# Batched x times y transposed on one core: longer DMA runs, 64-column weight tiles, deeper load prefetch, permutations moved to the transposed operands

## The chip, the core and the metric

The kernel runs on one core of one Trainium2 chip. The metric is device microseconds (us) of one execution; the median of three runs is given. A core has five engines: TensorE (PE, matmuls and transposes), VectorE (DVE), ScalarE (ACT), GpSimd (POOL) and SyncE (SP, which only issues transfers here). Sixteen DMA engines move data between HBM and the on-chip memory SBUF. Matmul results land in PSUM and are copied from there by DVE or ACT.

## The reference

```python
batch, n_heads, seq_t, seq_s, channels = 8, 12, 512, 512, 64      # x, y float32
np.einsum('bhtc,bhsc->bhts', x, y).astype(np.float32)
```

For each of 96 heads the output is a 512 x 512 float32 matrix, x times y transposed over 64 channels. Inputs are 12.6 MB each, the output is 100.7 MB.

## The kernel before, in words

The 96 heads are worked off in 24 groups of four (the loop at line 50). Everything below happens once per group, written out in program order; each engine takes its own instructions in that order, and waits are inserted where one needs another's result or a buffer that is still in use. Buffers rotate: three of each kind for loaded inputs, converted inputs, transposed inputs and outputs, four PSUM buffers for transposes and four for matmuls.

*Loads (lines 54 and 57, issued by SP).* Rows of a head are dealt out so that partition p holds the four consecutive rows 4p to 4p+3. One load brings 512 KB of x or y, as runs of 1 KB: four rows of 64 channels of 4 bytes, for 128 partitions and four heads.

*Conversion (lines 65 and 66, ACT).* Float32 becomes bf16. The heads of a pair are laid side by side, so that a 128-column block holds row 4p+tl of both heads.

*Transposes (lines 73 and 77, PE; copies at 74 and 78, DVE).* Each 128 x 128 block is turned over by PE into PSUM and copied to `xT` or `yT` by DVE. The first head of a pair then has its 64 channels on partitions 0 to 63, the second on 64 to 127. There are 16 transposes and 16 copies of 128 elements per partition in a group.

*Matmuls (line 87, PE).* For each head and each of four row sets there is one matmul: a 64 x 128 weight tile from `xT`, and all 512 columns of `yT`. That makes 16 per group, each filling one PSUM buffer of 128 x 512. In program order two heads of a pair follow each other, so the array rows 0 to 63 are used by four matmuls, then rows 64 to 127 by four.

*Output copies (line 96 on ACT, line 98 on DVE, alternating).* The columns of a matmul come in the order (sl, ps), while the output wants ps outside and sl inside. The copy from PSUM to `ot` undoes that: it reads in order and writes every fourth word.

*Store (line 99, issued by POOL).* One transfer of 4 MB per group, in runs of 8 KB: four rows of 512 columns per partition and head. It waits until all 16 copies of its group are done.

Of the kernel before, what the change touches and what calls it, by code (L numbers as in the profile page):

```python
# [1 line left out]

# [5 lines left out]


@with_exitstack
def kernel(
    ctx: ExitStack,
    tc: tile.TileContext,
    x: bass.AP,
    y: bass.AP,
    out: bass.AP,
):
    nc = tc.nc
    B, H, T, C = x.shape  # L20
    _, _, S, _ = y.shape
    BH = B * H
    P = 128
    TL = T // P
    SL = S // P
    fp32 = mybir.dt.float32
    bf16 = mybir.dt.bfloat16

    assert C * 2 == P

    NPAIR = 2
    BB = NPAIR * 2
    NB = BH // BB

    xv = x.rearrange("b h (p tl) c -> (b h) p tl c", p=P)
    yv = y.rearrange("b h (p sl) c -> (b h) p sl c", p=P)
    ov = out.rearrange("b h (p tl) s -> (b h) p tl s", p=P)

    const = ctx.enter_context(tc.tile_pool(name="const", bufs=1))
    ident = const.tile([P, P], bf16)  # L40
    make_identity(nc, ident)

    lpool = ctx.enter_context(tc.tile_pool(name="lpool", bufs=3))
    bpool = ctx.enter_context(tc.tile_pool(name="bpool", bufs=3))
    tpool = ctx.enter_context(tc.tile_pool(name="tpool", bufs=3))
    opool = ctx.enter_context(tc.tile_pool(name="opool", bufs=3))
    ptpool = ctx.enter_context(tc.tile_pool(name="ptpsum", bufs=4, space=bass.MemoryType.PSUM))
    pmpool = ctx.enter_context(tc.tile_pool(name="pmpsum", bufs=4, space=bass.MemoryType.PSUM))

    for nb in range(NB):  # L50
        bh0 = nb * BB
        xs = lpool.tile([P, BB, TL, C], fp32)
        ys = lpool.tile([P, BB, SL, C], fp32)
        nc.sync.dma_start(
            xs, xv[bh0:bh0 + BB].rearrange("bb p tl c -> p bb tl c")
        )
        nc.sync.dma_start(
            ys, yv[bh0:bh0 + BB].rearrange("bb p sl c -> p bb sl c")
        )
        xb = bpool.tile([P, NPAIR, TL, 2, C], bf16)  # L60
        yb = bpool.tile([P, NPAIR, SL, 2, C], bf16)
        for pr in range(NPAIR):
            xsv = xs[:, 2 * pr:2 * pr + 2].rearrange("p two tl c -> p tl two c")
            ysv = ys[:, 2 * pr:2 * pr + 2].rearrange("p two sl c -> p sl two c")
            nc.scalar.activation(xb[:, pr], xsv, mybir.ActivationFunctionType.Copy)  # L65
            nc.scalar.activation(yb[:, pr], ysv, mybir.ActivationFunctionType.Copy)  # L66

        xT = tpool.tile([P, NPAIR, TL, P], bf16)
        yT = tpool.tile([P, NPAIR, SL, P], bf16)
        for pr in range(NPAIR):  # L70
            for tl in range(TL):
                pt = ptpool.tile([P, P], bf16)
                nc.tensor.transpose(pt, xb[:, pr, tl, :, :], ident)  # L73
                nc.vector.tensor_copy(xT[:, pr, tl, :], pt)  # L74
            for sl in range(SL):
                pt = ptpool.tile([P, P], bf16)
                nc.tensor.transpose(pt, yb[:, pr, sl, :, :], ident)  # L77
                nc.vector.tensor_copy(yT[:, pr, sl, :], pt)  # L78

        ot = opool.tile([P, BB, TL, S], fp32)  # L80
        for pr in range(NPAIR):
            for two in range(2):
                bb = pr * 2 + two
                yTf = yT[two * C:(two + 1) * C, pr].rearrange("c sl p -> c (sl p)")
                for tl in range(TL):
                    pm = pmpool.tile([P, S], fp32)
                    nc.tensor.matmul(  # L87
                        pm,
                        xT[two * C:(two + 1) * C, pr, tl, :],
                        yTf,  # L90
                        start=True, stop=True,
                    )
                    pmv = pm.rearrange("p (sl ps) -> p sl ps", sl=SL)
                    otv = ot[:, bb, tl, :].rearrange("p (ps sl) -> p sl ps", sl=SL)
                    if tl % 2 == 0:
                        nc.scalar.activation(otv, pmv, mybir.ActivationFunctionType.Copy)  # L96
                    else:
                        nc.vector.tensor_copy(otv, pmv)  # L98
        nc.gpsimd.dma_start(  # L99
            ov[bh0:bh0 + BB].rearrange("bb p tl s -> p bb tl s"), ot  # L100
        )


# [1 line left out]
_INS = ['x', 'y']  # L105
_OUTS = [((8, 12, 512, 512), 'float32')]


# [23 lines left out]
```

## Time and profile before

| | us |
|---|---|
| median of three runs (321.52, 322.62, 323.64) | 322.62 |
| profiled execution, span from first to last instruction | 323.1 |

| | |
|---|---|
| loads | 48, of 512 KB |
| stores | 24, of 4 MB |
| HBM read / written | 25.17 MB / 100.66 MB |
| mean rate over the span | 390 GB/s |
| instructions | 2677 |

How to read the lines that follow in this document. Busy rows give microseconds and the share of the span for each engine; PEld is PE's weight loads. A group row has line, engine, operation, output and input tiles with shape, then a count, total busy time, mean ns of one, and the idle time before it with what ended it. A timeline row has start, duration, engine, line, operation and a count of instructions merged into the row. A window row has the stretch and its length, the busy time of PE, PEld, DVE, ACT and POOL with instruction counts, the granted share of the TensorE clock, the DMA share (mean busy share of the 16 DMA engines; over 1 where packets of one engine overlap) and GB/s. A queue row has packets, MB and the time that its packets took as a share of 16 engines' span. q1 carries what SP issues, q0 what POOL issues. Ends of matmuls are modelled, starts are recorded.

### The profile page before, as it was taken

How to read it: one execution, taken by the hardware profiler on the slowest of the kernel's cores; microseconds unless marked ns; L12 is line 12 of the kernel's file. 1: busy time of each engine (PE TensorE's matmuls, PEld its weight loads, DVE VectorE, ACT ScalarE, POOL GpSimd, SP SyncE). 2: the span in 40 equal slices, each digit the busy share in tenths (PEclk: the TensorE clock that was granted, in tenths of full speed). 3: DMA queues.
4: the chain of work that ended last, by engine and by line, in shares of the span. 5: the costliest groups of instructions: out<-in, count | busy, mean ns of one | idle time of the engine just before them, and what ended most of it. 6: DMA issues, size and time to landing. Idle time of an engine off the chain costs nothing. (4 is left out here: it accounts for less than half of the span.)

```text
span 323.1 us, 2677 instructions
## 1 busy us (share of the span) xinstructions
PE 235.5 (73%) x768; PEld 76.6 (24%) x768; DVE 237.3 (73%) x576; ACT 233.3 (72%) x289; POOL 18.7 (6%) x30
## 2 busy tenths in 40 slices
PE   2578878878386697787887877977966999889300
PEld 1122222224032213313312313312312223222000
DVE  2488797797287877877886886886867899999500
ACT  4798678684669688687697697696686976699400
POOL 0010000000000000000000000000000000000000
DMA  7959999999999999999999999999998699999995
GB/s 249 353 180 405 365 420 419 421 422 417 410 331 406 349 424 415 417 420 417 409 428 417 411 426 415 415 426 417 420 425 350 290 418 392 397 402 414 417 422 247
DMA packets 38031, 126.01 MB, mean 390 GB/s; under 512 B 1152, under 2 KB 25728, under 8 KB 25728
## 3 DMA queue, kind: packets, MB, share of 16 engines
q0 software_dynamic: 12672, 100.66, 74.5%
q1 hardware_dynamic: 25344, 25.17, 23.0%
q8 instruction: 6, 0.10, 0.1%
q14 instruction: 9, 0.07, 0.1%
HBM read 25.17 MB, written 100.66 MB: 389 GB/s over the span
## 5 line engine op out<-in xcount | busy, mean ns | idle before, releaser
L87 PE MATMUL pm<-yT,xT 64*128 64x512 bf16 x384 | 179.7, 603 | 54.3 <-ACT ot L96 51.2
L98 DVE COPY ot<-pm 128x512 f32<-128x512 f32 x192 | 184.4, 1080 | 36.4 <-PE pm L87 36.2
L96 ACT ACTIVATE ot<-pm 128x512 f32<-128x512 f32 x192 | 184.4, 1119 | 12.2 <-PE pm L87 12.1
L87 PEld LDWEIGHTS <-xT 64*128 64x128 bf16 x384 | 38.7, 111 | 166.8 <-issue 130.7
L65 ACT ACTIVATE xb<-xs 128x512 bf16<-128x512 f32 x48 | 28.6, 629 | 48.1 <-PE pt L73 25.7
L78 DVE COPY yT<-pt 128x128 bf16<-128x128 bf16 x192 | 30.8, 218 | 23.7 <-PE pt L77 23.7
L77 PE MATMUL pt<-ident,yb 128*128 128x128 bf16 x192 | 32.6, 283 | 7.1 <-DVE xT L74 6.3
L73 PE MATMUL pt<-ident,xb 128*128 128x128 bf16 x192 | 32.4, 271 | 4.9 <-ACT xb L65 4.9
L66 ACT ACTIVATE yb<-ys 128x512 bf16<-128x512 f32 x48 | 28.6, 629 | 8.3 <-DMA ys<-in_y_dram 7.0
L99 POOL DMA_DIRECT2D out_dram<-ot x24 | 18.0, 752 | 285.1 <-DVE xT L74 208.1
L74 DVE COPY xT<-pt 128x128 bf16<-128x128 bf16 x192 | 29.8, 226 | 5.8 <-PE pt L73 5.8
L77 PEld LDWEIGHTS <-yb 128*128 128x128 bf16 x192 | 18.5, 114 | 35.6 <-issue 31.0
L73 PEld LDWEIGHTS <-xb 128*128 128x128 bf16 x192 | 20.2, 111 | 22.1 <-issue 12.1
L65 ACT ACT_TABLE_LOAD x1 | 1.3, 1283 | 0.7 <-PEq L116 0.7
masks.py:199 POOL TENSOR_SCALAR_AFFINE_SELECT ident<-ident 128x128 bf16<-128x128 bf16 x1 | 0.3, 290 | 0.1
masks.py:197 POOL MEMSET ident<- 128x128 bf16 x1 | 0.2, 205 | 0.3 <-POOLq L116 0.3
L116 POOL MEMSET const-float32-0.0<- 128x1 f32 x1 | 0.1, 99 | 0.2 <-issue 0.2
L116 POOL MEMSET const-bfloat16-1.0<- 128x1 bf16 x1 | 0.1, 102 | 0.0
L116 POOL MEMSET const-uint8-127<- 128x1 uint8 x1 | 0.1, 102 | 0.0
L116 POOL MEMSET const-float32-1.0<- 128x1 f32 x1 | 0.1, 99 | 0.0
## 6 DMA issues: line engine op xcount, KB each, us to landing
out_dram<-ot POOLq DMA_DIRECT2D x24, 4096.0 KB, 15.9
xs<-in_x_dram SPq DMA_DIRECT2D x24, 512.0 KB, 12.7
ys<-in_y_dram SPq DMA_DIRECT2D x24, 512.0 KB, 14.6
```

Of the source, the lines that this page charges most:

```text
L65: nc.scalar.activation(xb[:, pr], xsv, mybir.ActivationFunctionType.Copy)
L66: nc.scalar.activation(yb[:, pr], ysv, mybir.ActivationFunctionType.Copy)
L73: nc.tensor.transpose(pt, xb[:, pr, tl, :, :], ident)
L74: nc.vector.tensor_copy(xT[:, pr, tl, :], pt)
L77: nc.tensor.transpose(pt, yb[:, pr, sl, :, :], ident)
L78: nc.vector.tensor_copy(yT[:, pr, sl, :], pt)
L87: nc.tensor.matmul(pm, xT[two * C:(two + 1) * C, pr, tl, :], yTf, start=True, stop=True,)
L96: nc.scalar.activation(otv, pmv, mybir.ActivationFunctionType.Copy)
L98: nc.vector.tensor_copy(otv, pmv)
L99: nc.gpsimd.dma_start(ov[bh0:bh0 + BB].rearrange("bb p tl s -> p bb tl s"), ot)
L116: nc = _bacc.Bacc("TRN2", target_bir_lowering=False, num_devices=1)
```

## The change

The group stays four heads, with a different deal of rows. A load is read as a flat 512 KB: partition p gets 4 KB, 16 consecutive rows of head p // 32. A store covers two heads, 2 MB; each partition writes eight consecutive output rows, 16 KB.

Weight tiles have 64 columns: 32 partitions of a head times two row octets. Each matmul fills 64 partitions of a PSUM buffer that is now 128 x 2 x 512, so two heads and two row parities, four matmuls, share a buffer. Even rows have their channels on partitions 0 to 63 and odd rows on 64 to 127. The columns of y are needed on both halves, so y is written twice side by side in the conversion and transposed in 16 blocks, x in 8. The order of columns and rows is put right in the copies of transposed blocks (three copies of 128 x 1024 per group, two on DVE and one on ACT); the output copies read and write in order, 1024 elements at a time.

Conversions move from ACT to POOL. All transfers are issued by SP, loads for six groups ahead of everything else, then each group's loads behind the conversion that frees their buffers. Buffers: six for loads, two for converted and transposed inputs, eight for outputs, two PSUM buffers for transposes and three for matmuls. The preparation of the next group is a generator whose steps are interleaved with the output tiles of the present one. The first and the last output tile are stored in two halves.

The deleted loop is the one printed above; the new code:

```diff
-    xv = x.rearrange("b h (p tl) c -> (b h) p tl c", p=P)
-    yv = y.rearrange("b h (p sl) c -> (b h) p sl c", p=P)
-    ov = out.rearrange("b h (p tl) s -> (b h) p tl s", p=P)
+    G = 4
+    Q = P // G
+    R = T // Q
+    NG = B * H // G
+    K = R // 2
+    HP = 2
+    I = R // 2
...
+    xv = x.rearrange("b h t c -> (b h t c)").rearrange("(g p n) -> g p n", p=P, n=R * C)
+    yv = y.rearrange("b h t c -> (b h t c)").rearrange("(g p n) -> g p n", p=P, n=R * C)
+    ov = out.rearrange("b h t s -> (b h t s)").rearrange("(g a p n) -> g a p n", a=G // HP, p=P, n=I * S)
...
+    lpool = ctx.enter_context(tc.tile_pool(name="lpool", bufs=6))
+    bpool = ctx.enter_context(tc.tile_pool(name="bpool", bufs=2))
+    tpool = ctx.enter_context(tc.tile_pool(name="tpool", bufs=2))
+    opool = ctx.enter_context(tc.tile_pool(name="opool", bufs=8))
+    ptpool = ctx.enter_context(tc.tile_pool(name="ptpsum", bufs=2, space=bass.MemoryType.PSUM))
+    pmpool = ctx.enter_context(tc.tile_pool(name="pmpsum", bufs=3, space=bass.MemoryType.PSUM))
+
+    loaded = {}
+
+    def load(g):
+        xs = lpool.tile([P, R * C], fp32)
+        ys = lpool.tile([P, R * C], fp32)
+        nc.sync.dma_start(ys, yv[g])
+        nc.sync.dma_start(xs, xv[g])
+        loaded[g] = (xs, ys)
+
+    for g in range(6):
+        load(g)
...
+    def prepare(g, made):
+
+        xs, ys = loaded.pop(g)
+        yb = bpool.tile([P, R, 2, C], bf16)
+        nc.gpsimd.tensor_copy(
+            yb, ys.rearrange("p (r c) -> p r c", c=C).unsqueeze(2).to_broadcast([P, R, 2, C])
         )
+        xb = bpool.tile([P, R * C], bf16)
+        nc.gpsimd.tensor_copy(xb, xs)
+        if g + 6 < NG:
+            load(g + 6)
+        yield
+        yT = tpool.tile([P, G * Q, R], bf16)
+        xT = tpool.tile([P, K // 2, P, 2], bf16)
+        for half in range(2):
+            pt = ptpool.tile([P, K, P], bf16)
+            for k in range(K):
+                nc.tensor.transpose(
+                    pt[:, k, :], yb[:, half * K + k].rearrange("p a c -> p (a c)"), ident
+                )
+            dst = yT[:, :, half * K:(half + 1) * K]
+            src = pt.rearrange("p k n -> p n k")
+            if half == 0:
+                nc.vector.tensor_copy(dst, src)
+            else:
+                nc.scalar.activation(dst, src, mybir.ActivationFunctionType.Copy)
+            yield
+        pt = ptpool.tile([P, K, P], bf16)
+        for k in range(K):
+            nc.tensor.transpose(pt[:, k, :], xb[:, k * P:(k + 1) * P], ident)
+        nc.vector.tensor_copy(
+            xT.rearrange("p i n e -> p i e n"), pt.rearrange("p (e i) n -> p i e n", e=2)
         )
+        made[g] = (xT, yT.rearrange("p n k -> p (n k)"))
+        yield
...
+    made = {}
+    for _ in prepare(0, made):
+        pass
+    for g in range(NG):
+        xT, yT = made.pop(g)
+        steps = prepare(g + 1, made) if g + 1 < NG else iter(())
+        for hp in range(G // HP):
+            ot = opool.tile([P, I, S], fp32)
+            edge = (g == 0 and hp == 0) or (g == NG - 1 and hp == 1)
+            for i2 in range(I // 2):
+                if i2 % 2 == 0:
+                    next(steps, None)
+                pm = pmpool.tile([P, 2, S], fp32)
+                for h2 in range(HP):
+                    h = hp * HP + h2
+                    for par in range(2):
+                        nc.tensor.matmul(
+                            pm[h2 * 64:(h2 + 1) * 64, par, :],
+                            xT[par * C:(par + 1) * C, i2, h * Q:(h + 1) * Q, :].rearrange("c q e -> c (q e)"),
+                            yT[par * C:(par + 1) * C, h * S:(h + 1) * S],
+                            start=True, stop=True,
+                        )
+                if i2 % 2 == 0:
+                    nc.scalar.activation(ot[:, 2 * i2:2 * i2 + 2, :], pm, mybir.ActivationFunctionType.Copy)
+                else:
+                    nc.vector.tensor_copy(ot[:, 2 * i2:2 * i2 + 2, :], pm)
+                if edge and i2 % 2 == 1:
+                    a, b = (2 * i2 - 2) * S, (2 * i2 + 2) * S
+                    nc.sync.dma_start(ov[g, hp][:, a:b], ot.rearrange("p r s -> p (r s)")[:, a:b])
+            if not edge:
+                nc.sync.dma_start(ov[g, hp], ot.rearrange("p r s -> p (r s)"))
```

More of the change, by code (lines that the diff above doesn't have):

```diff
@@ L21 @@
     _, _, S, _ = y.shape
-    BH = B * H
     P = 128
-    TL = T // P
-    SL = S // P
+    G = 4
[5 more added lines that the diff above has]
+    I = R // 2
     fp32 = mybir.dt.float32
     bf16 = mybir.dt.bfloat16
[L29 to L33, printed above, removed]
-    xv = x.rearrange("b h (p tl) c -> (b h) p tl c", p=P)
-    yv = y.rearrange("b h (p sl) c -> (b h) p sl c", p=P)
-    ov = out.rearrange("b h (p tl) s -> (b h) p tl s", p=P)
@@ L39 @@
-    const = ctx.enter_context(tc.tile_pool(name="const", bufs=1))
+    assert C * 2 == P and S == T and R == 16
+    xv = x.rearrange("b h t c -> (b h t c)").rearrange("(g p n) -> g p n", p=P, n=R * C)
+    yv = y.rearrange("b h t c -> (b h t c)").rearrange("(g p n) -> g p n", p=P, n=R * C)
+    ov = out.rearrange("b h t s -> (b h t s)").rearrange("(g a p n) -> g a p n", a=G // HP, p=P, n=I * S)
+    const = ctx.enter_context(tc.tile_pool(name="const", bufs=1))
+    lpool = ctx.enter_context(tc.tile_pool(name="lpool", bufs=6))
@@ L40 @@
+    for g in range(6):
+        load(g)
     ident = const.tile([P, P], bf16)
     make_identity(nc, ident)
[L43 to L55, printed above, removed]
-        )
-        nc.sync.dma_start(
-            ys, yv[bh0:bh0 + BB].rearrange("bb p sl c -> p bb sl c")
-        )
[L60 to L101, printed above, removed]
```

## The prediction

> **What bounds the kernel now.** I read the page's totals first, then its slices and DMA queues.
>
> ```profile
> PE 235.5 (73%) x768; PEld 76.6 (24%) x768; DVE 237.3 (73%) x576; ACT 233.3 (72%) x289; POOL 18.7 (6%) x30
> ...
> DMA packets 38031, 126.01 MB, mean 390 GB/s; under 512 B 1152, under 2 KB 25728, under 8 KB 25728
> ...
> q0 software_dynamic: 12672, 100.66, 74.5%
> q1 hardware_dynamic: 25344, 25.17, 23.0%
> ```
>
> No compute engine passes 73%, while the two queues take 97.5% of the 16 DMA engines' time. Each transfer ends in a small packet per engine (1152 in all), so q0 has 12672 - 384 = 12288 data packets of 8 KB and q1 25344 - 768 = 24576 of 1 KB. In queue time one 8 KB packet costs 0.745 x 16 x 323.1 / 12288 = 313.4 ns, one 1 KB packet 0.230 x 16 x 323.1 / 24576 = 48.4 ns. Summed and spread over 16 engines that is 315.0 us of the 323.1.
>
> Then the windows: busy time of each engine, granted clock, DMA share and GB/s.
>
> ```profile
> 0.00:2.40 2.40, 0.00 (x0) 0.00 (x0) 0.00 (x0) 1.28 (x1) 0.70 (x6) 1.00 0.13 29
> 5.00:18.00 13.00, 8.15 (x32) 2.77 (x33) 6.90 (x21) 9.93 (x16) 0.00 (x0) 1.00 1.06 344
> 18.00:23.50 5.50, 3.91 (x14) 1.28 (x12) 5.07 (x16) 5.50 (x10) 0.88 (x1) 1.00 0.46 143
> 204.00:219.00 15.00, 12.23 (x39) 3.78 (x37) 12.25 (x31) 11.22 (x14) 0.83 (x2) 1.00 1.02 421
> 240.00:260.00 20.00, 16.95 (x60) 5.92 (x58) 16.30 (x46) 15.30 (x18) 1.49 (x2) 1.00 0.81 338
> 304.00:319.00 15.00, 0.00 (x0) 0.00 (x0) 0.00 (x0) 0.00 (x0) 0.45 (x1) 1.00 1.00 416
> 319.00:323.10 4.10, 0.00 (x0) 0.00 (x0) 0.00 (x0) 0.00 (x0) 0.00 (x0) 1.00 0.21 86
> ```
>
> Nothing moves for 2.4 us at the start. At the end 86 GB/s over 4.1 us is 0.35 MB, 0.8 us of work, so some 3.3 us are empty. Between them are stretches of 344 GB/s with 1 KB loads alone, 421 with both kinds, 416 with 8 KB stores alone, and holes. The first hole, 18.0 to 23.5, follows three groups of loads: input buffers are full, and the first store only goes out at 22.41. The later one (240 to 260, 338 GB/s) comes when no loads are left to fill the time between stores. In the timeline of that phase:
>
> ```profile
> 22.41 0.88 POOL L99 DMA_DIRECT2D out_dram<-ot  x1 [21.11 <-DVE yT L78]
> ...
> 259.62 7.47 DVE L98 COPY ot<-pm 128x512 f32<-128x512 f32 x8
> 260.59 6.88 ACT L96 ACTIVATE ot<-pm 128x512 f32<-128x512 f32 x7 [2.23 <-PE pm L87]
> 262.57 3.68 PE L87 MATMUL pm<-yT,xT 64*128 64x512 bf16 x8 [0.23 <-DVE ot L98]
> 267.63 0.75 POOL L99 DMA_DIRECT2D out_dram<-ot  x1 [9.79 <-DVE xT L74]
> 278.00 0.75 POOL L99 DMA_DIRECT2D out_dram<-ot  x1 [9.62 <-DVE xT L74]
> ```
>
> Stores leave 10.37 us apart, while 4.19 MB at 416 GB/s take 10.1: there compute sets the pace. So the time is DMA work first and compute where its slack has run out. Both matter for the change.
>
> **The change, part by part.** *DMA run lengths.* Bytes stay; packets become 6144 loads of 4 KB and 6144 stores of 16 KB. Through my two prices goes a line of (313.4 - 48.4) / 7168 = 0.0370 ns per byte plus 10.5 ns per packet. It gives 162.0 ns for 4 KB (between two measured sizes) and 616.3 ns for 16 KB (beyond them). The sum is 6144 x (162.0 + 616.3) / 16 = 298.9 us, 16.1 less than 315.0; loads give 12.1 of it, stores 4.0. Two independent rows fit the prices: 416 GB/s alone is 315 ns per 8 KB, and 344 GB/s at a share of 1.06 is 48 ns of wall per 1 KB. The only 16 KB packets of this trace are instruction fetches:
>
> ```profile
> q8 instruction: 6, 0.10, 0.1%
> ```
>
> At 0.1% of 16 x 323.1 us, six of them took roughly 0.9 us each, beside store traffic. That is the dear bound; the cheap one is that packets overlap as in the rows with shares of 1.02, 298.9 / 1.02 = 293.0 us. I take the line, since stores alone run at a share of 1.00.
>
> *Ends and holes.* 2.4 us and 3.3 us stay. The first hole should close: six groups are requested at once, a seventh while the first is prepared. Per group the loads cost 256 x 162.0 / 16 = 2.6 us, so DMA is fed until 2.4 + 7 x 2.6 = 20.6. The first store, now half of a two-head tile, can be ready before that; the landing of the first inputs and the small POOL operations give its date:
>
> ```profile
> 4.25 0.63 ACT L65 ACTIVATE xb<-xs 128x512 bf16<-128x512 f32 x1 [2.23 <-DMA xs<-in_x_dram]
> 5.72 0.63 ACT L66 ACTIVATE yb<-ys 128x512 bf16<-128x512 f32 x1 [0.84 <-DMA ys<-in_y_dram]
> ...
> masks.py:199 POOL TENSOR_SCALAR_AFFINE_SELECT ident<-ident 128x128 bf16<-128x128 bf16 x1 | 0.3, 290 | 0.1
> masks.py:197 POOL MEMSET ident<- 128x128 bf16 x1 | 0.2, 205 | 0.3 <-POOLq L116 0.3
> L116 POOL MEMSET const-float32-0.0<- 128x1 f32 x1 | 0.1, 99 | 0.2 <-issue 0.2
> ```
>
> *POOL.* It now converts 2048 + 1024 elements per partition and group. The trace shows no conversion there. From 1 to 128 elements a memset grows 106 ns and the select 191 over the memset of one element: 0.83 and 1.50 ns per element, so 2.6 to 4.6 us per group. I take 4.6, as a copy reads like the select does. It no longer waits for stores. The Trainium skill's page "GPSIMD Engine Reference" (section 3.1) measures about 2.6 cycles per element for a two-input add at 1.2 GHz, and section 4.1 advises against elementwise work there; by that figure, an estimate, a group would take 6.7 us. No run here shows a conversion on POOL; the sum would be the same by either.
>
> *Copies on DVE and ACT.*
>
> ```profile
> 268.29 0.62 DVE L78 COPY yT<-pt 128x128 bf16<-128x128 bf16 x4 [0.78 <-PE pt L77]
> 159.42 1.15 ACT L65 ACTIVATE xb<-xs 128x512 bf16<-128x512 f32 x2 [2.77 <-issue]
> ```
>
> Today's output copies write every fourth word and cost 7.47 / 8 = 0.93 us per 512 on DVE, 0.98 on ACT. The new ones write in order. In-order writes cost 0.155 us per 128 on DVE and (1.15 - 0.63) = 0.52 per 512 on ACT. For 1024 elements: DVE between 1.24 and 1.87, ACT between 1.04 and 1.97. I take the low ends, the rows with in-order writes. The permutation moves into the copies of transposed x and y (1024 elements each, strided reads or writes); I give these the high ends, and note that strided PSUM reads are not in the trace. Per group DVE does 4 x 1.24 + 2 x 1.87 = 8.7 us, ACT 4 x 1.04 + 1.97 = 6.1; with strided prices throughout 11.2 and 9.8.
>
> *PE.* Transposes go from 16 to 24 per group, matmuls from 16 to 32, each with 64 weight columns and 512 moving columns.
>
> ```profile
> 15.98 0.61 PE L87 MATMUL pm<-yT,xT 64*128 64x512 bf16 x2
> 159.25 0.66 PE L77 MATMUL pt<-ident,yb 128*128 128x128 bf16 x4
> 259.75 0.27 PE L73 MATMUL pt<-ident,xb 128*128 128x128 bf16 x1
> L87 PE MATMUL pm<-yT,xT 64*128 64x512 bf16 x384 | 179.7, 603 | 54.3 <-ACT ot L96 51.2
> L87 PEld LDWEIGHTS <-xT 64*128 64x128 bf16 x384 | 38.7, 111 | 166.8 <-issue 130.7
> ```
>
> Matmuls on the same rows of the array follow at about (3.68 - 0.60) / 7 = 0.44 us. The first row here is the pair in program order where the rows change from 64-127 to 0-63: two take the time of one. The change alternates rows at each matmul. If only such pairs overlap, 16 x 0.44 = 7.0 us; if column halves overlap too, 3.5; if nothing does, 14.1. Transposes at (0.66 - 0.27) / 3 = 0.13 add 3.1; weight loads at half of 0.111, if none hides, 1.8. So 6.6 to 11.9 us, and 19.0 without any overlap. I take pairs with half the loads hidden, 11.0. The skill's page "TensorEngine Tiling (Array Packing)" (section Tiling Modes) says that different tiles run matmuls and weight loads in parallel, and that changing the mode drains the engine, which speaks against three blocks of transposes per group among tiled matmuls. The 15.98 row agrees on rows; no run here shows column tiles, and by the page PE would need 6.6 us and the drains.
>
> *Does compute keep up?* DMA needs 298.9 / 24 = 12.45 us per group with loads, 256 x 616.3 / 16 = 9.86 without. While loads run, every estimate lies under 12.45, so stores pile up: with eight output tiles of 4.9 us each, seven can stand ahead of the one in transfer, 34 us. In the last six groups PE at 11.0 is late by 1.1 each, 7 us, paid from the lead. Hence compute costs nothing. The date of the first store: y at 4.3 (now loaded first), conversions to 4.3 + 4.6 = 8.9, three blocks of eight transposes with copies about 5, two output tiles 2.5, so about 16.5 against 20.6.
>
> *SP.*
>
> ```profile
> 160.59 0.37 SPq L54 DMA_DIRECT2D xs<-in_x_dram  x1
> L99 POOL DMA_DIRECT2D out_dram<-ot x24 | 18.0, 752 | 285.1 <-DVE xT L74 208.1
> ```
>
> It issues 48 loads and 50 stores (0.37 us each, 36 us in all) where POOL issued 24 at 0.75. Loads of a later group wait for POOL's conversion, and the store behind them in program order waits with them. That is covered by transfers already queued; a POOL late by more than the queue's backlog would leave DMA empty.
>
> Sum: 2.4 + 298.9 + 3.3 = 304.6. The same account for before gives 320.7 against its 323.1, the rest being holes less overlaps. The profiled span is within 0.5 us of the median, 322.6. I predict **304.5 us**.
>
> **The rivals.** (1) *More overlap*: 293.0 + 5.7 = 298.7. For it: shares of 1.02 to 1.06; against: 1.00 with stores alone. (2) *Run length buys little*: long descriptors are cut, or bytes and not packets cost. With stores still cut at 8 KB, 6144 x 162.0 / 16 + 240.7 + 5.7 = 308.6; with loads unchanged as well, 315.0 + 5.7 = 320.7. For it: the line rests on two sizes and 16 KB lies outside; against: 344 beside 416 GB/s. (3) *Matmuls don't overlap*: PE at 19.0 us per group becomes the bound, 16 + 24 x 19.0 + 5 = 477; without exposed weight loads 433. It decides from 12.6 us per group, where 20 + 24 x 12.6 equals today's time. For it: column tiles are nowhere in the trace; against: the 15.98 row. (4) *POOL conversion is the bound*: needs over 12.6 / 3072 = 4.1 ns per element; at three times the select's slope, 4.5, it is 20 + 24 x 13.8 = 351. Against: both POOL rows. (5) *The strided copies are*: DVE needs (12.6 - 5.0) / 2 = 3.8 us for each, twice my price; at 4.0 it is 20 + 24 x 13.0 = 332.
>
> **How the numbers follow.** A measurement here tells about 1% from no change, 319.4 to 325.8. Chances: forecast (301 to 309) 0.62, rival 1 0.08, rival 2 0.15 (0.12 of it below 319.4, 0.03 within 1%), rival 3 0.06, rival 4 0.05, rival 5 0.04 (half of it within 1%). Faster 0.82, same 0.05, slower 0.13. The range leaves out the slower cases and the top of rival 2: 298 to 316, with rival 1 at its low end.
>
> **What would show it.** Right: 4 KB packets near 162 ns and 16 KB near 616 in queue time, a DMA share of at least 0.98 from 3 us to the end, no hole at 18 to 23, a first store before 20.6, output copies near 1.2 and 1.0 us, PE pairs starting together. Wrong: more than 12288 data packets, a share that falls while PE, POOL or DVE is full, or SP's stores waiting behind a load for POOL.

## The result and the profile after

The changed kernel takes 308.95 us, the median of four runs (306.84 to 309.27), beside 322.19 for the kernel before, timed with it: a ratio of 0.955, 95% interval 0.949 to 0.961. The profiled run is one of 308.88 us with a span of 307.1, so 1.8 us lie around the span. I had predicted 304.5 within 298 to 316. Direction and cause hold; the time is 4.4 us longer than the sum.

First the page of the changed kernel: totals, DMA and GB/s in 40 slices, packets and queues.

```profile
PE 154.7 (50%) x1344; PEld 82.8 (27%) x1344; DVE 172.9 (56%) x144; ACT 117.3 (38%) x121; POOL 70.6 (23%) x54
...
DMA  7999999999999999999999999999999999999970
GB/s 277 415 400 438 420 418 429 419 436 414 423 436 416 425 428 428 425 426 423 433 428 417 437 427 424 430 425 431 428 427 433 428 425 438 429 427 435 430 327 42
DMA packets 14127, 126.04 MB, mean 410 GB/s; under 512 B 1568, under 2 KB 1568, under 8 KB 7712
...
q1 hardware_dynamic: 14112, 125.84, 97.4%
q8 instruction: 10, 0.16, 0.2%
```

The holes are gone: after the first slice the rate stays at 400 GB/s or more until the last two. Queue time is 0.974 x 307.1 = 299.1 us; the line through the two old packet sizes had said 298.9. Now the windows that answer to those of before.

```profile
5.00:18.00 13.00, 10.45 (x92) 6.36 (x93) 8.54 (x8) 5.58 (x6) 10.54 (x8) 1.00 1.02 404
18.00:23.50 5.50, 4.61 (x56) 2.41 (x56) 5.50 (x6) 4.81 (x6) 2.88 (x2) 1.00 1.03 399
40.00:240.00 200.00, 113.61 (x948) 61.67 (x948) 122.04 (x102) 80.73 (x85) 49.76 (x34) 0.59 1.01 426
```

The last stretch in the kernel before:

```profile
40.00:240.00 200.00, 154.06 (x518) 52.09 (x517) 154.89 (x395) 151.15 (x194) 11.19 (x15) 1.00 1.02 412
```

Loads alone run at 404 GB/s instead of 344, the hole at 18.0 to 23.5 has 399 instead of 143, and the long middle 426 instead of 412. The groups of instructions show the engines with time to spare (after the bar: busy us and mean ns of one):

```profile
L125 DVE COPY ot<-pm 128x1024 f32<-128x1024 f32 x96 | 116.4, 1220 | 80.8 <-DMA out_dram<-ot 60.1
L123 ACT ACTIVATE ot<-pm 128x1024 f32<-128x1024 f32 x96 | 94.3, 1022 | 144.1 <-DMA out_dram<-ot 131.6
L68 POOL CAST yb<-ys 128x2048 bf16<-128x2048 f32 x24 | 45.4, 1893 | 138.9 <-DMA ys<-in_y_dram 108.9
L94 DVE COPY xT<-pt 128x1024 bf16<-128x1024 bf16 x24 | 31.1, 1298 | 9.5 <-PE pt L93 9.5
L87 DVE COPY yT<-pt 128x1024 bf16<-128x1024 bf16 x24 | 29.1, 1214 | 7.1 <-PE pt L81 7.1
L72 POOL CAST xb<-xs 128x1024 bf16<-128x1024 f32 x24 | 25.0, 1040 | 21.6 <-PE pt L93 21.6
L89 ACT ACTIVATE yT<-pt 128x1024 bf16<-128x1024 bf16 x24 | 24.7, 1028 | 7.0 <-PE pt L81 6.2
```

ACT, DVE and POOL mostly wait for a store or a load: DMA sets the pace. What the sum had missed is at the end. Here are the last stretches in 40 slices each, first of the kernel before (311 to 323.1, 0.30 us a slice), then of the changed one (295 to 309, 0.35 us a slice).

```profile
GB/s 406 379 406 406 433 433 406 433 406 433 433 433 433 433 433 433 433 433 406 433 406 433 433 433 379 433 433 379 379 54 27 0 0 0 0 0 0 0 0 0
```

```profile
GB/s 468 398 445 304 375 281 304 234 70 140 70 117 117 140 94 47 70 47 47 70 47 70 47 23 23 23 23 23 47 23 0 0 0 0 0 0 0 0 23 0
DMA packets 196, 1.47 MB, mean 105 GB/s; under 512 B 31, under 2 KB 31, under 8 KB 31
```

Before, all 16 DMA engines stop within a microsecond. After, they stop one by one: 23 is one 8 KB packet per slice, one engine at work. Spread evenly, at the 428 GB/s of the stretch from 240 to 260 us, the 1.47 MB would have ended at 295 + 1.47 / 0.428 = 298.4; the last engine ends at 295 + 30 x 0.35 = 305.5. That costs 7.1 us.

### The profile page after: what moved, and what is told of

Same layout as the page of the kernel before. It is cut to its first block, busy times and chain, and to the rows that moved or that the text cites. A ratio compares the mean times of both kernels' runs of the same rounds, so it can differ in the third digit from the quotient of the medians.

```text
span 307.1 us, 3408 instructions
## 1 busy us (share of the span) xinstructions
PE 154.7 (50%) x1344; PEld 82.8 (27%) x1344; DVE 172.9 (56%) x144; ACT 117.3 (38%) x121; POOL 70.6 (23%) x54
## 4 chain that ended last, share of the span: by engine, by line
DMA 78%; DVE 5%; PE 3%; issue 1%; ACT 1%; POOL 1%; SPq 0%; ACTq 0%
DMA out_dram<-ot 77%; DVE ot L125 3%; PE pm L116 1%; DVE xT L94 1%; DMA ys<-in_y_dram 1%; PE pt L81 1%; DVE yT L87 1%; ACT ot L123 1%; POOL yb L68 1%; PE pt L93 0%; SPq L130 0%; ACTq L123 0%
## 5 line engine op out<-in xcount | busy, mean ns | idle before, releaser
L125 DVE COPY ot<-pm 128x1024 f32<-128x1024 f32 x96 | 116.4, 1220 | 80.8 <-DMA out_dram<-ot 60.1
L123 ACT ACTIVATE ot<-pm 128x1024 f32<-128x1024 f32 x96 | 94.3, 1022 | 144.1 <-DMA out_dram<-ot 131.6
L116 PE MATMUL pm<-yT,xT 64*64 64x512 bf16 x768 | 95.1, 556 | 91.0 <-ACT ot L123 72.3
L68 POOL CAST yb<-ys 128x2048 bf16<-128x2048 f32 x24 | 45.4, 1893 | 138.9 <-DMA ys<-in_y_dram 108.9
L116 PEld LDWEIGHTS <-xT 64*64 64x64 bf16 x768 | 32.1, 120 | 138.8 <-issue 120.5
L81 PEld LDWEIGHTS <-yb 128*128 128x128 bf16 x384 | 34.6, 128 | 24.6 <-issue 18.2
L94 DVE COPY xT<-pt 128x1024 bf16<-128x1024 bf16 x24 | 31.1, 1298 | 9.5 <-PE pt L93 9.5
L87 DVE COPY yT<-pt 128x1024 bf16<-128x1024 bf16 x24 | 29.1, 1214 | 7.1 <-PE pt L81 7.1
L72 POOL CAST xb<-xs 128x1024 bf16<-128x1024 f32 x24 | 25.0, 1040 | 21.6 <-PE pt L93 21.6
L89 ACT ACTIVATE yT<-pt 128x1024 bf16<-128x1024 bf16 x24 | 24.7, 1028 | 7.0 <-PE pt L81 6.2
```

The lines of the kernel that those rows point to most:

```text
L68: nc.gpsimd.tensor_copy(yb, ys.rearrange("p (r c) -> p r c", c=C).unsqueeze(2).to_broadcast([P, R, 2, C]))
L72: nc.gpsimd.tensor_copy(xb, xs)
L81: nc.tensor.transpose(pt[:, k, :], yb[:, half * K + k].rearrange("p a c -> p (a c)"), ident)
L87: nc.vector.tensor_copy(dst, src)
L89: nc.scalar.activation(dst, src, mybir.ActivationFunctionType.Copy)
L94: nc.vector.tensor_copy(xT.rearrange("p i n e -> p i e n"), pt.rearrange("p (e i) n -> p i e n", e=2))
```

## The experiments

The theory after the result: the time is the packets' queue time, spread over 16 engines, plus what the slowest engine is late; compute, buffers and queues are covered. Rivals: the gain comes from prefetch depth, from the cheaper copies, or from the queue. The ratio is to the kernel before, timed beside each run. Timed together were store_8k, load_1k, more_pe and less_pe; control, load_1k_one, before_deep and wide_load; and the other four.

| run | us | ratio, 95% interval |
|---|---|---|
| control: the changed kernel again | 306.93 | 0.952, 0.949 to 0.955 |
| store_8k | 311.75 | 0.963, 0.956 to 0.969 |
| load_1k: four transfers per load | 335.98 | 1.039, 1.031 to 1.048 |
| load_1k_one: one transfer per load | 314.62 | 0.977, 0.972 to 0.982 |
| before_deep: the kernel before, deep prefetch | 318.69 | 0.989, 0.986 to 0.992 |
| small_buf | 307.61 | 0.952, 0.947 to 0.956 |
| strided_out | 306.96 | 0.950, 0.945 to 0.956 |
| pool_store | 309.95 | 0.959, 0.954 to 0.964 |
| more_pe | 309.99 | 0.958, 0.952 to 0.964 |
| less_pe | 305.99 | 0.946, 0.939 to 0.954 |
| wide_load | 308.66 | 0.957, 0.954 to 0.960 |
| no_dup | 309.21 | 0.957, 0.951 to 0.963 |

**Control.** No edit. 

> The changed kernel itself again, as the yardstick on this chip. Expected 309 (306.8 to 309.3 so far).

 It came at 306.93; with the first runs that gives the changed kernel 307 to 309.

**Store runs undone.**

```diff
-            edge = (g == 0 and hp == 0) or (g == NG - 1 and hp == 1)
+            edge = True
```

> Every output tile is stored in two transfers, each of 8 KB runs instead of 16 KB; all else is as in the changed kernel. Theory (price per packet as on the line, 8 KB = 309 to 313 ns): store packets rise from 6144 to 12288, queue time by about (12288 x 311 - 5888 x 613 - 512 x 312) / 16 = 3.3 us, the time from 309 to about 312. Rival (the longer store run brings nothing, all gain comes from loads and holes): 309 within 0.5. Second rival (two stores per tile let DMA start earlier and waits shrink): below 308.

311.75 us, ratio 0.963 beside 0.952 and 0.955 for the changed kernel: 2.5 to 3.5 us of 323, near the 3.3 that the packet price gave. The run also issues 46 transfers more; what these cost by themselves it does not show. In the middle of the run (20 to 260 us) the rate is 420 GB/s:

```profile
20.00:260.00 240.00, 138.52 (x1200) 73.79 (x1198) 154.70 (x130) 102.80 (x107) 58.50 (x40) 0.62 1.01 420
```

and in the control, at the same place:

```profile
20.00:260.00 240.00, 139.40 (x1220) 74.19 (x1217) 157.44 (x132) 105.01 (x109) 58.40 (x40) 0.63 1.01 426
```

**Load runs undone, first try.** Four transfers of 1 KB runs for each load.

```diff
-        nc.sync.dma_start(ys, yv[g])
-        nc.sync.dma_start(xs, xv[g])
+        for j in range(4):
+            nc.sync.dma_start(ys[:, j * 256:(j + 1) * 256], yv[g][:, j * 256:(j + 1) * 256])
+        for j in range(4):
+            nc.sync.dma_start(xs[:, j * 256:(j + 1) * 256], xv[g][:, j * 256:(j + 1) * 256])
```

> Each 512 KB load is cut into four transfers of 128 runs of 1 KB, as long as the runs of the kernel before; stores stay at 16 KB. Theory (the load packets set most of the gain): 24576 x 48.4 instead of 6144 x 163.4 ns over 16 engines is 74.3 instead of 62.7 us, so 11.6 us more, about 320.5. Rival (loads of 1 KB are cheap once they lie ahead in one queue with stores, packets overlapping): under 313. Issue time on SP grows by 144 x 0.33 = 48 us and should be hidden by six groups of lead.

336 us, beyond both. SP issues one transfer in 0.46 us at the start, and 128 KB per 0.46 us is 285 GB/s, so SP and not DMA sets the first 20 us. The timeline of SP and the window 5 to 20 us:

```profile
0.74 1.81 SPq L55 DMA_DIRECT2D ys<-in_y_dram  x4
```

```profile
5.00:20.00 15.00, 9.86 (x109) 6.02 (x110) 10.35 (x9) 7.36 (x8) 10.43 (x7) 1.00 0.83 260
```

That explains about 6 of the 29 us: from 2.4 to 20 us the rate was 261 GB/s against 407 in the control. Later 16 KB packets took 641 instead of 613 ns, for which no run here gives the reason. The run does not price the run length; it shows that my "issue time is hidden by the lead" fails while no lead exists yet.

**Load runs undone, second try.** One transfer, four pieces of 1 KB per partition.

```diff
-    xv = x.rearrange("b h t c -> (b h t c)").rearrange("(g p n) -> g p n", p=P, n=R * C)
+    xv = x.rearrange("b h t c -> (b h t c)").rearrange("(g j p n) -> g p j n", j=4, p=P, n=R * C // 4)
...
-        nc.sync.dma_start(xs, xv[g])
+        nc.sync.dma_start(xs.rearrange("p (j n) -> p j n", j=4), xv[g])
```

> Each load stays one transfer of 512 KB, but reads four pieces of 1 KB per partition that lie 128 KB apart in HBM. So packets are 1 KB and SP issues no more transfers than in the changed kernel. Rows are dealt out in another order by this, so output rows come permuted; all other work is the same. The run with four transfers per load mixed two things: 128 KB per issue at about 0.45 us of SP each held the first 20 us to 261 GB/s, and packets of 16 KB took 641 instead of 613 ns. Theory (packet price alone): queue time 74.3 instead of 62.7 us for loads, 11.6 us more than the control, about 320.5. Rival A (1 KB loads also stretch the 16 KB stores that share their ring, 28 ns on each of 5888, 10 us): about 330. Rival B (loads ahead in the queue overlap and cost little): under 313.

314.62, so 7.7 us over the control: between theory (11.6) and rival B (under 313). Queue and windows:

```profile
q1 hardware_dynamic: 32544, 125.84, 99.7%
```

```profile
5.00:18.00 13.00, 9.47 (x92) 5.70 (x96) 8.50 (x8) 6.04 (x6) 10.71 (x8) 1.00 1.07 341
20.00:260.00 240.00, 136.94 (x1188) 73.55 (x1185) 153.99 (x129) 102.37 (x107) 58.40 (x40) 0.62 1.02 415
```

The queue and the first window of the control (its second stands above):

```profile
q1 hardware_dynamic: 14112, 125.84, 98.0%
```

```profile
5.00:18.00 13.00, 9.56 (x88) 5.83 (x88) 8.34 (x7) 6.04 (x6) 10.70 (x8) 1.00 1.02 412
```

The queue time is 0.997 x 312.9 = 312.0 us, 13.0 more than the control's 0.980 x 305.1 = 299.0; even more than the price said. But short packets overlap (shares 1.07 and 1.02 against 1.02 and 1.01 in the control). Spread evenly, the bytes would have ended at 307.2 us against the control's 298.2, 9.0 later, and the last engine is a little less late (4.3 against 5.2 us), which leaves about the 7.7 us measured. Rival A falls: 16 KB packets took 616 ns here.

**Prefetch alone, in the kernel before.** Six input and four output buffers, loads six groups ahead.

```diff
-    lpool = ctx.enter_context(tc.tile_pool(name="lpool", bufs=3))
+    lpool = ctx.enter_context(tc.tile_pool(name="lpool", bufs=6))
-    opool = ctx.enter_context(tc.tile_pool(name="opool", bufs=3))
+    opool = ctx.enter_context(tc.tile_pool(name="opool", bufs=4))
...
+    for nb in range(6):
+        load(nb)
...
+        if nb + 6 < NB:
+            load(nb + 6)
```

> The kernel before with one part of the change alone: six input buffers instead of three, loads issued six groups ahead (the next one behind the conversion of a group), four output buffers instead of three. Run lengths, tiles, copies and queues stay. Theory (the time is queue time of packets, 315 us, and the hole at 18 to 23 us only let DMA engines fall behind what they had to do anyway): 318 to 322, little changed, and the engines no longer end together. Rival (the holes were the loss, 9 us at 421 GB/s): 311 to 314.

318.69, 4.0 us less than before: within the theory's span, and far from the rival's 311 to 314. The engines end together here too (the rate falls from 442 GB/s to nothing within 1 us), against the theory's last clause.

**Buffers undone in the changed kernel.**

```diff
-    lpool = ctx.enter_context(tc.tile_pool(name="lpool", bufs=6))
+    lpool = ctx.enter_context(tc.tile_pool(name="lpool", bufs=3))
-    opool = ctx.enter_context(tc.tile_pool(name="opool", bufs=8))
+    opool = ctx.enter_context(tc.tile_pool(name="opool", bufs=3))
...
-    for g in range(6):
+    for g in range(3):
...
-        if g + 6 < NG:
-            load(g + 6)
+        if g + 3 < NG:
+            load(g + 3)
```

> The deep prefetch is undone: three input buffers and loads three groups ahead instead of six, three output buffers (2 MB each) instead of eight. All else as in the changed kernel. Theory (once running, DMA is fed by two stores in flight and loads ahead; only the start suffers, since three groups of loads last until 2.4 + 3 x 2.6 = 10 us and the first store comes at 15): 3 to 6 us more than the control's 307, and engines that end closer together because compute waits for the slowest at every tile. Rival (depth carries the gain): back to 318 or more. Second rival (depth is without effect): 307.

307.61, 0.7 over the control and over strided_out, which was timed beside it. My 3 to 6 us at the start are wrong: conversions free the buffers early. The next five loads go out between 6.0 and 12.8 us, two of them before the first three groups have run out, and the first store at 13.25. The windows 2.4 to 10 and 10 to 20 us:

```profile
2.40:10.00 7.60, 2.90 (x24) 2.47 (x24) 1.75 (x2) 1.02 (x1) 4.80 (x4) 1.00 1.00 366
10.00:20.00 10.00, 8.90 (x85) 4.32 (x86) 8.70 (x8) 6.43 (x7) 6.67 (x5) 1.00 1.03 395
```

In the control the two windows have 400 and 412 GB/s, so the start costs about 1 us. Depth, worth 4 us in the old kernel, is worth under 1 in the new one. My reading, not tested apart: tiles of two heads are ready sooner, and POOL, not the busy ACT, frees the inputs.

**Permutations put back into the output copies.**

```diff
+                pmv = pm.rearrange("p r (sl ps) -> p r sl ps", sl=4)
+                otv = ot[:, 2 * i2:2 * i2 + 2, :].rearrange("p r (ps sl) -> p r sl ps", sl=4)
-                    nc.scalar.activation(ot[:, 2 * i2:2 * i2 + 2, :], pm, mybir.ActivationFunctionType.Copy)
+                    nc.scalar.activation(otv, pmv, mybir.ActivationFunctionType.Copy)
-                    nc.vector.tensor_copy(ot[:, 2 * i2:2 * i2 + 2, :], pm)
+                    nc.vector.tensor_copy(otv, pmv)
```

> The output copies write every fourth word again, as before the change (128 x 2 x 512 elements in each, words 16 bytes apart), so output columns come permuted; everything else as in the changed kernel. It asks what the move of the permutations is worth by itself. From the kernel before, a copy of 1024 should cost 1.87 on DVE and 1.96 on ACT; DVE 4 x 1.87 + 2.5 = 10.0 and ACT 4 x 1.96 + 1.0 = 8.9 us per four heads. Theory (DMA needs 12.4 us per four heads with loads, 9.8 without, and there are eight output tiles of lead): 307 to 309, the move alone is worth next to nothing while runs are long and buffers many. Rival (compute becomes the bound, as it was in the last phase of the kernel before): 313 or more.

306.96: no loss, although the copies cost twice as much on ACT (2012 against 1022 ns) and 1.6 times as much on DVE (1981 against 1220).

```profile
L125 ACT ACTIVATE ot<-pm 128x1024 f32<-128x1024 f32 x96 | 185.0, 2012 | 56.7 <-DMA out_dram<-ot 32.3
L127 DVE COPY ot<-pm 128x1024 f32<-128x1024 f32 x96 | 183.4, 1981 | 14.7 <-PE pm L116 12.0
```

DVE is at 236.0 us of 305.2 and still behind DMA. The cheaper copies give slack, not time.

**Stores back on POOL's queue.** `nc.sync.dma_start(ov[g, hp]...)` becomes `nc.gpsimd.dma_start(ov[g, hp]...)` at both places.

> Stores are issued by POOL again, loads by SP, as before the change; runs, tiles, copies and buffers as in the changed kernel. Theory (the two queues share the same 16 DMA engines, and POOL has 230 us idle): packets keep their price, 306 to 309. Rival A (POOL waits for each tile's copies ahead of the next conversion, compute loses its lead): 312 or more. Rival B (two rings per engine overlap packets better than one, as shares of 1.02 to 1.03 before suggested): below 304.

309.95, just above the theory's range: 3.0 us over the control, 2.3 and 3.0 over small_buf and strided_out, which were timed beside it, and 1.0 over the first result. Because the queues are apart here, packet prices can be read by size:

```profile
q0 software_dynamic: 7200, 100.67, 76.5%
q1 hardware_dynamic: 6912, 25.17, 20.5%
```

A 4 KB load is 0.205 x 16 x 308.4 / 6144 = 165 ns. Of the 7200 packets 800 are small ends and 512 are 8 KB (at 0.311 us, 159 us together); the other 5888 take (0.765 x 16 x 308.4 - 159) / 5888 = 0.614 us. The line had said 162 and 616. The middle is as fast as on one queue (427 GB/s from 100 to 200 us here and in the control), so rival B falls; the loss is in the last stretch (295 to 309 us), where one engine is alone from slice 15 on:

```profile
GB/s 445 398 398 398 468 351 328 304 234 187 140 94 47 47 23 23 23 23 23 23 47 23 23 23 23 23 23 47 0 0 0 0 0 0 0 0 0 0 0 0
DMA packets 201, 1.47 MB, mean 105 GB/s; under 512 B 29, under 2 KB 29, under 8 KB 29
```

The last packet ends at 295 + 28 x 0.35 = 304.8 us, 1.4 later than the control's 303.4 (its slices stand below). Then 3.6 us pass until the span ends at 308.4, against 1.7 in the control. The other two runs that store through POOL have 2.7 (the kernel before) and 2.8 (before_deep) there. So issuing stores from SP shortens the empty end by 1 to 2 us.

The Trainium skill's page "DMA: Bandwidth & Descriptors" (Rules for kernel authors) says that spreading transfers over issuing engines gains no bandwidth, since all run on the same 16 DMA engines. This run agrees: 427 GB/s in the middle with two queues and with one.

**More and fewer instruction fetches.** In more_pe the block of four matmuls stands in `for again in range(2):`. In less_pe one matmul of 128 columns serves two heads and half of y's transposes are left out:

```diff
-                for h2 in range(HP):
-                    h = hp * HP + h2
-                    for par in range(2):
...
+                for par in range(2):
+                    nc.tensor.matmul(
+                        pm[:, par, :],
+                        xT[par * C:(par + 1) * C, i2, hp * HP * Q:(hp + 1) * HP * Q, :].rearrange("c q e -> c (q e)"),
+                        yT[par * C:(par + 1) * C, hp * HP * S:(hp * HP + 1) * S],
+                        start=True, stop=True,
+                    )
```

> Each block of four matmuls is issued twice into the same PSUM tile, so results stay and PE gets 1536 more instructions, six more 16 KB instruction fetches. Theory (the long tail of the changed kernel, one DMA engine alone at the end, comes from instruction fetches that fall on one or two engines and delay their stores by 1.3 us each): three to four more on the slowest engine, so the last store lands 4 to 5 us later, about 313 to 314, while queue time of data packets stays 299. Rival (engines differ in speed, or the tail is the last transfers' own shape): 309 within 0.5, as PE would still be under 85% busy.

> Left out: the transposes of the second half of the rows of y (the copy takes the first half again), and the products of each second head with its own y (one matmul of 128 weight columns serves two heads with the first head's y). PE has 1152 instructions fewer, 4 or 5 fetches fewer; all transfers and copies stay. Theory of the instruction fetches: two to three fewer on the slowest engine, the tail shorter by 2.6 to 4 us, about 305 to 306. Rival (engines differ in speed): 309 within 0.5, with the same tail of one engine alone.

309.99 and 305.99 us: more_pe comes near the rival's 309 and far from 313 to 314, less_pe falls where the theory had it. Fetches of 16 KB (queue q8 carries the program's own instructions) and the last stretch, of more_pe:

```profile
q8 instruction: 16, 0.26, 0.3%
```

```profile
GB/s 421 445 398 375 328 304 234 304 304 234 257 164 140 70 94 94 0 47 0 23 23 47 23 23 23 23 23 23 47 23 23 23 23 0 0 0 0 0 0 0
DMA packets 216, 1.61 MB, mean 115 GB/s; under 512 B 32, under 2 KB 32, under 8 KB 32
```

and of less_pe:

```profile
q8 instruction: 6, 0.10, 0.1%
```

```profile
GB/s 492 375 398 445 304 258 257 211 94 117 117 70 70 23 23 23 47 23 23 0 0 0 0 0 0 0 23 0 0 0 0 0 0 0 0 0 0 0 0 0
DMA packets 168, 1.19 MB, mean 85 GB/s; under 512 B 26, under 2 KB 26, under 8 KB 26
```

The control, with ten fetches like the profiled run after the change:

```profile
GB/s 468 398 468 351 328 304 211 257 94 117 94 117 94 117 70 47 70 47 70 47 47 47 47 47 0 0 0 0 0 0 0 0 23 0 0 0 0 0 0 0
DMA packets 189, 1.39 MB, mean 99 GB/s; under 512 B 30, under 2 KB 30, under 8 KB 30
```

Against an even end (295 plus the rest of the bytes at 0.428 MB per us) the last engine is late by 306.6 - 298.8 = 7.8 us with 16 fetches, 7.1 with 10 and 301.7 - 297.8 = 3.9 with 6. These three go the theory's way, though six more fetches brought 0.7 us instead of 4 to 5. The other runs with ten fetches do not fit in: 303.4 - 298.2 = 5.2 in the control, 5.1 in strided_out, 4.4 in small_buf, 304.8 - 298.4 = 6.4 in pool_store (one engine late, the others nearly even), and only 1.5 in load_1k. With nine, no_dup is late by 8.5. So the number of fetches does not set how late the last engine is.

The lateness is not made at the end either. Each transfer closes with 16 small packets, one for each engine, and the trace has the time at which each landed. In the control the last of them comes 0.9 us after the first at 10 us, 3.4 at 100, 5.7 at 200, and 7.5 from 265 us on. In the profiled run after the change, the latest falls from 0.8 to 2.1 us behind the middle of the 16 between 19.5 and 22 us, where a fetch of 1.1 us lies at 20.1, and from 6.7 to 8.2 around the fetch at 218.0; the second latest falls behind in small steps, from 2.3 us at 107 to 5.5 at 269. So a fetch can show as a step, and ground is also lost between fetches.

**Two versions meant to gain more.** no_dup transposes y once and writes both partition halves by half copies:

```diff
-        yb = bpool.tile([P, R, 2, C], bf16)
+        yb = bpool.tile([P, R * C], bf16)
+        nc.gpsimd.tensor_copy(yb, ys)
...
+        for side in range(2):
+            for par in range(2):
+                dst = yT[side * C:(side + 1) * C].rearrange("c n (k two) -> c n k two", two=2)[:, :, :, par]
+                src = pt[par * C:(par + 1) * C].rearrange("c k n -> c n k")
```

> The changed kernel with y converted and transposed once, in 8 blocks instead of 16, and written to both partition halves by four copies of 64 partitions x 1024 (two on DVE, two on ACT) instead of two of 128. Loads, stores and buffers stay. PE issues 384 instructions fewer, one or two 16 KB fetches fewer; DVE rises to about 4 x 1.22 + 1.3 + 2 x 1.22 = 8.6, ACT to 4 x 1.02 + 2 x 1.25 = 6.6 us per four heads, both under 9.8. Theory: 1 us below the control at best, 305.5 to 307. Rival (DVE at 8.6 is too slow in the first 40 us, where no lead has formed, as in the version with wide loads, where xT copies of 2.44 us and a load queued behind four stores on SP left 336 to 362 GB/s): 308 or more.

wide_load does that with loads of eight heads (G = 8, R = 32, three input buffers, seven output buffers, xT with four row octets beside each other); its PE issues 192 pairs of weight load and matmul fewer, half of y's transposes.

> A version that carries two findings further. Loads take eight heads, 1 MB with 8 KB runs, three such groups ahead; y is transposed once, in 16 blocks per eight heads, and the copies from PSUM write it to both partition halves (64 partitions by 1024 elements, four per four heads, one on DVE and three on ACT). PE has 768 transposes and matmuls fewer by 192 of its 1344 pairs, 384 instructions in all, and POOL converts 2048 instead of 3072 elements per four heads. Seven output buffers. Theory: loads 3072 x 311 instead of 6144 x 163 ns over 16 engines saves 3.0 us, one or two instruction fetches fewer save about 1: 305. Rival 1 (longer load packets only delay the first store; no packets saved matter): 309. Rival 2 (ACT and DVE at about 7.3 us per four heads leave too little lead near the end, where DMA needs 9.8): above 309.

Neither beats the control: 309.21 and 308.66. In no_dup it is mostly the slow end that grew (8.5 us late against 5.2); an even end would come 0.9 later. In wide_load the loads do run faster at first (422 GB/s from 2.4 to 20 us against 407), but the 3.0 us of queue time were not saved in all: 0.976 x 306.6 = 299.2 us, beside the control's 299.0. And two early stretches of low rate, 25 to 35 and 45 to 55 us, cost 3.7 us against 426 GB/s:

```profile
25.00:35.00 10.00, 6.16 (x60) 3.73 (x60) 8.93 (x6) 9.65 (x10) 2.89 (x2) 0.68 0.87 349
45.00:55.00 10.00, 6.99 (x64) 3.85 (x64) 8.96 (x7) 8.77 (x9) 2.82 (x2) 0.62 1.01 345
```

In the first, DVE and ACT are full (8.9 and 9.7 of 10 us) and the DMA share falls to 0.87: no lead has formed yet, and one copy became dear (below). In the second the share reads 1.01, so there packets took longer, and why is not shown. What I had weighed was the average load per four heads; the loss lay in the first 60 us.

## Why the prediction was right, and where it was off

*DMA sets the time, run lengths cut it.* Right, and shown for the larger part: undoing load runs costs 7.7 us, store runs 2.5 to 3.5, out of 15.8 (322.70 to 306.93, timed together). Of the rest the queue of the stores accounts for 1 to 3 us by pool_store, 1 to 2 of them in the empty end, which I had not priced. That these parts add up was not tried. Packet prices outside and inside the measured sizes came out within 2% (616 against 614 ns, 162 against 165).

*The sum.* Its failed step is "summed and spread over 16 engines": it takes queue time for wall time and lets all engines end together. Two errors of opposite sign came of it. Packets overlap at a share of 1.01, so the bytes would have been moved evenly by 298.4 us, 2.9 earlier than my 2.4 + 298.9 = 301.3. And the last engine ends 7.1 us after that, which the sum had at nothing. Of my 3.3 us of empty end 1.6 remain, as stores no longer go through POOL. 298.4 + 7.1 + 1.6 is the span of 307.1. The other 1.8 us lie between span and time. I had taken them as next to nothing, because the profiled span of the old kernel, 323.1, lay near the median of other executions; its timed runs have 1.8 to 1.9 there too (322.86 us with a span of 321.0). So the errors are -2.9, +7.1, -1.7 and +1.8, 4.3 in all, and that they cancel in part is luck. The same step overvalued the loads: 12.1 us of queue time, 7.7 of time. Of the signs that I had named, the DMA share of at least 0.98 to the end is the one that failed: 0.88 from 260 to 304 us.

*Holes.* I gave them 2.4 us in all (323.1 against an account of 320.7). Deep prefetch with a fourth output buffer gains 4.0 in the old kernel. In the new kernel they stay closed with three buffers, but for about 1 us at the start, and also with strided copies and eight buffers; both undone at once was not tried.

*First store.* Predicted 16.5 us, issued at 15.2; DMA was fed until then, as reckoned.

*Covered work.* Right in kind, too dear in size. POOL takes 1.89 + 1.04 = 2.9 us per group (I took 4.6; the low end of 2.6, from the memset, was nearer), the copies that permute 1.21, 1.30 and 1.03 (I took 1.87 and 1.97), the in-order output copies 1.22 and 1.02 as predicted. PE needs 154.7 / 24 = 6.4 us per group instead of 11.0, near the bound where column tiles overlap too. Rivals 3, 4 and 5 are far away.

*What stays open.* Why the engines drift apart, by 1.5 to 8.5 us at the end of runs with 16 KB stores. Instruction fetches share the engines with stores, and some fetches show as steps of 1.3 to 1.5 us in the landings, but their number does not order the runs. The records do not say which engine a packet ran on, so the cause is not settled. In the kernel before and in before_deep the end is even; in those compute still left gaps near the end, in which a late engine could catch up, but that was only argued. load_1k speaks against it as the whole reason: its 16 landings stay within 2.5 us of each other all the way, at a DMA share of 0.98 to 1.01 after the first 20 us.

Not undone by themselves are the 64-column weight tiles, the move of the conversions to POOL, and the interleaving of a group's preparation with the output of the one before.

## What to carry to other kernels

When DMA is full, price each transfer by packets (a fixed part and a part per byte) rather than by bytes; here one line through two sizes gave the others within 2%. Then take two things off the sum before believing it: short packets overlap, so their queue time is more than their wall time, and the kernel ends with its slowest DMA engine, not with the mean one. Undoing parts singly showed that two of them (deep buffers, moved permutations) bring under 1 us beside the run lengths, though they look like the bulk of the edit.

## What the runs showed of the hardware

Four 64 x 64 tiles of the matmul array work at once, and the clock column needs care. Timeline of PE in the changed kernel, early and late:

```profile
10.74 1.06 PE L116 MATMUL pm<-yT,xT 64*64 64x512 bf16 x8 [0.70 <-DVE xT L94]
16.97 0.63 PE L116 MATMUL pm<-yT,xT 64*64 64x512 bf16 x8
161.26 0.64 PE L116 MATMUL pm<-yT,xT 64*64 64x512 bf16 x4 [0.41 <-DVE ot L125]
```

Four matmuls take 0.64 us at 161.26, as long as one of them by itself (0.63). Eight take 1.06 us at 10.74 and 0.63 at 16.97, though the clock column reads 1.00 at both; at 161.26 it reads 0.5. The trace has no record of the clock before 16.8 us, so the 1.00 ahead of that is not full speed. The kernel before has no such record at all, and its column reads 1.00 throughout: there no matmul took less than 0.58 us, and on the same rows they followed at 0.44, while from 30 to 60 us in the changed kernel one takes 0.37 to 0.40. So the 1.00 of the kernel before was not full speed. The Trainium skill's page "TensorE: Matmul & The Clock Gate" (Part 1) says that half rate is the default and sustained activity releases it. The changed kernel agrees in part: half rate until 16.8 us, full rate from there to 61.2 (PE busy for 28.86 of 44.2 us), mostly half after that (112.77 of 199 us to 260). The kernel before kept the pace of half rate although PE was busy for 73% of its span, so the busy share alone does not decide it here.

In these copies write strides set the price, PSUM read strides did not. Copies that read PSUM 256 bytes apart and write runs of 16 bytes took 1.21 us per 1024; 2-byte writes 4 bytes apart took 1.30, and 8 bytes apart, in wide_load, nearly twice as much:

```profile
L96 DVE COPY xT<-pt 128x1024 bf16<-128x1024 bf16 x24 | 58.6, 2443 | 29.6 <-PE pt L95 29.5
```
